# Last pair's small copies moved from GpSimd to VectorE and ScalarE, its transposes put ahead of its products, and more projections held back

## The chip, the cores and the metric

The kernel runs on one core of a Trainium2 chip. The metric is the device time of one execution in microseconds (us): the median of three runs, beside one further execution that was profiled. A profiled execution gives, for each instruction of each engine, its start and its length; all places below are us from the start of that span.

## The reference, cut to what matters

A sequence of 512 positions with 1024 channels goes through two blocks of two layers each, in float32. Only the first block is touched.

```python
h = rms_norm(x, norm_g) * (1 + scale) + shift
a_qkv, a_z, m_cq, m_ckv, m_kr, m_z, merge = split(h @ w_in)
y_a = dilated_mixer(a_qkv, rel_bias) * silu(a_z)      # 3 groups x 8 heads
y_m = mla_mixer(m_cq, m_ckv, m_kr, ...) * silu(m_z)   # 16 heads, causal
g_a, g_m = split(sigmoid(merge))
merged = g_a * (y_a @ w_out_a) + g_m * (y_m @ w_out_b)
x = x + gate * (merged @ w_o)
```

In `dilated_mixer` each of 8 heads has three attentions (window and stride 128/1, 512/4, 2048/16) whose results are mixed by a softmax over their three log-sums. So the weight of each probability needs a small exchange between the three groups, whose queries lie in different orders.

## The kernel before, in words

Every product with a weight matrix is made in three float32r passes (high x high, high x low, low x high: lines 259 to 261), and so one projection of 128 columns over 1024 channels is 24 MATMULs of 128x512, "24 products" below. Weights come as a stream of chunks of up to 1024 columns (512 KB) by DMAs that SyncE issues (line 1642) into four raw buffers. ScalarE casts a chunk to its high part (line 1658) and VectorE makes the low part (line 1659), three chunks ahead of their use. The load of chunk n+4 waits until both have read chunk n. Some chunks (`w_ada`, 32 of them in the first layer's attention) are no weights for TensorE: VectorE reduces each by itself (line 642, 1024 columns).

The order of the program is fixed when it is built. `Order.weave` merges three streams of items: `sc` (scores, softmax, and the small exchange), `tm` (scaling, transposes, products with the values) and `fill` (projections that TensorE can do meanwhile). An item may say that it comes at least so much planned time behind another (`after`); among those that are ready the stream that is furthest behind its share goes first. `hold` counts for `fill` as work already done, so a larger `hold` leaves more projections for the end. Each engine runs its own instructions strictly in that order.

The first weave of a layer is the dilated attention: four pairs of heads (`hp` 0 to 3). For each pair:

- four `scores` items (matmuls in line 795, VectorE's bias and maximum in line 801, ScalarE's exponentials in line 807);
- `combine`: `gather` (18 small copies between partitions, lines 819 and 822, GpSimd), `weigh` and `share` (lines 829 to 843, small VectorE work and one exponential), and 17 small copies back (lines 844 and 847, GpSimd);
- `scale` (line 861, VectorE, multiplies the probabilities by the copied factors), `turn` (transposes, line 870, copied out in line 872 by VectorE or ScalarE) and `mix` (products with the values, line 890).

The fill of this weave holds the next pair's projections, the first heads of the second attention (`heads(0)` and `heads(1)`, with four GpSimd additions in line 1004 that need VectorE's line 571, and copies in lines 1001 and 1008) and five gate projections. In the first layer, `bias_rows2` follows the weave: one DMA of 4088 KB between two DRAM tables, issued by GpSimd (line 605, `rows<-dt`).

The second weave is the second attention (MLA), eight pairs `j` of heads: scores (line 1036), `scale` (1053), `turn` (1061, copied out in 1063), `mix` (1074), the last step of a pair in line 1078. Behind it come the splits of the eight results (`split_ym`, lines 239 and 240), and then for each of 8 blocks a gate projection and the product with `w_out_b`.

Of the kernel before, what the change touches and what calls it, by code (L numbers as in the profile page):

```python
# [17 lines left out]
P = 128  # L18
S = 512
D = 1024  # L20
KD = D // P
DEPTH = 2
NEG = -1e30
HOLD = 20000
NG = 5
DC = 1500
DF = 6000
DT = 5000
# [31 lines left out]
O_MG = O_MZ + 1024  # L60
# [129 lines left out]
class Kernel:  # L190
# [479 lines left out]
    def first_layer(self, l):  # L670
        nc = self.nc
        st = self.st
        get = lambda name: (lambda inputs: inputs[name][l])
        w_in = get("w_in")
# [133 lines left out]
            return Item(1300, fn)  # L808


        def combine(hp):
            v5 = lambda x: x.rearrange("p (v g h b) -> p v g h b", v=2, g=3, h=2)
            v4 = lambda x: x.rearrange("p (g h b) -> p g h b", g=3, h=2)

            def gather(_):
                u = st["u", hp] = self.small(48)
                uv, ml = v5(u), v5(st["ml", hp])
                for v in range(2):
                    nc.gpsimd.tensor_copy(uv[:, v, 0], ml[:, v, 0])
                for b in range(4):  # L820
                    for p in range(4):
                        nc.gpsimd.tensor_copy(uv[32 * p:32 * p + 32, :, 1:3, :, b], ml[32 * b:32 * b + 32, :, 1:3, :, p])

            def weigh(_):
                uv = v5(st["u", hp])
# [8 lines left out]
            def share(_):  # L834
                uv, e = v5(st.pop(("u", hp))), st.pop(("e", hp))
                le, s = self.small(24), self.small(8)
                nc.vector.tensor_tensor(v4(le), uv[:, 1], v4(e), ALU.mult)
                nc.vector.tensor_tensor(s, le[:, 0:8], le[:, 8:16], ALU.add)
                nc.vector.tensor_tensor(s, s, le[:, 16:24], ALU.add)
                nc.vector.reciprocal(s, s)  # L840
                cf = st["cf", hp] = self.small(24)
                cv, ev = v4(cf), v4(e)
                nc.vector.tensor_tensor(ev, ev, s.rearrange("p (h b) -> p h b", h=2).unsqueeze(1).to_broadcast([P, 3, 2, 4]), ALU.mult)
                nc.gpsimd.tensor_copy(cv[:, 0], ev[:, 0])
                for b in range(4):
                    for p in range(4):
                        nc.gpsimd.tensor_copy(cv[32 * b:32 * b + 32, 1:3, :, p], ev[32 * p:32 * p + 32, 1:3, :, b])
            out = [Item(0, gather)]
            out.append(Item(0, weigh, after=[(out[0], 4000)]))
            out.append(Item(0, share, after=[(out[1], 1500)]))  # L850
            return out

# [74 lines left out]
        for hp in range(4):  # L927
# [8 lines left out]
            c[0].after.append((s[3], DC))  # L936
            t = {(h2, b): turn(hp, h2, b) for b in range(4) for h2 in range(2)}
            f = [scale(hp, b) for b in range(4)]
            f[0].after.append((c[-1], DF))
            for b in range(4):  # L940
                t[0, b].after.append((f[b], DT))
            m = [mix(hp, b) for b in range(4)]
# [27 lines left out]
    def first_rest(self, l, sc, tm, fill):  # L970
# [12 lines left out]
        def oa_evac(ps, f):  # L983
            y = self.t()
            self.gated(y, st.pop("sg"), ps)
            st["A", f] = y
            if f == 7:
                for i in range(4):
                    st.pop(("ya", i))
        out_a = []  # L990
        for f in range(8):
            out_a.append(self.proj(w_in, rng(O_MG + f * P, P), D, H, ga_evac) + self.proj(get("w_out_a"), rng(f * P, P), 512, lambda: [st["ya", i] for i in range(4)], lambda ps, f=f: oa_evac(ps, f)))
# [104 lines left out]
        for j in range(8):  # L1097
# [24 lines left out]
            m[3].after.append((gate[-1], MG))  # L1122
            tail[j] = m[3]
            sc += spaced(s, MS) + f
            tm += t[0]
            for k in range(4):
                tm += (t[k + 1] if k < 3 else []) + [m[k]]

        for j in range(6):
            first = next(i for i in fill if i is done[j + 2])  # L1130
# [2 lines left out]
        out = []  # L1133
# [4 lines left out]

        def ob_evac(ps, f):
            y = self.t()  # L1140
            self.gated(y, st.pop("sg"), ps)
            nc.vector.tensor_tensor(y, y, st.pop(("A", f)), ALU.add)
            st["mg"].append(self.split(y))
            if f == 7:
                st.pop("yms")
                st.pop("h")
# [3 lines left out]
            st["mg"] = []  # L1150
        out += [Item(0, split_ym), Item(0, begin)]
        for f in range(8):
            out += self.proj(w_in, rng(O_MG + D + f * P, P), D, H, ga_evac)
            out += self.proj(get("w_out_b"), rng(f * P, P), D, lambda: st["yms"], lambda ps, f=f: ob_evac(ps, f))

        def x_load(_):
# [585 lines left out]
```

## Time and profile before

| | |
|---|---|
| median of three runs | 3296.12 us (3291.93 to 3296.24) |
| profiled execution, its own time | 3293.89 us |
| its span | 3292.0 us |
| TensorE (PE) busy | 3222.0 us, 98% of the span |
| VectorE (DVE) busy | 1793.2 us, 54% |
| ScalarE (ACT) busy | 1272.4 us, 39% |
| GpSimd (POOL) busy | 394.0 us, 12% |
| mean DMA rate | 103 GB/s |

A row of the timeline reads: start in us, length in us, engine, line, operation, output<-input, shape, how many were merged into the row; in brackets the time that the engine stood idle before it and who ended that wait. A row of the waits names who waited for whom: us in total, times, longest. "PEclk" is the clock granted to TensorE, 1.00 for its full 2.4 GHz and 0.50 for 1.2 GHz.

### The profile page before, as it was taken

Reading aid. Unit: us, or ns where it says so; the run is one execution under the profiler, and the core shown is the slowest. Engines: PE = TensorE matmul, PEld = TensorE weight load, DVE = VectorE, ACT = ScalarE, POOL = GpSimd, SP = SyncE. Lnnn points to the kernel's source line nnn. Section 1 sums busy time; section 2 is a strip of 40 time slices with the busy share of each in tenths; the row PEclk is TensorE's granted clock in tenths of the full one; section 3 lists DMA queues with packets and bytes.
Section 4 is the critical chain, followed back from the end, with each engine's and each line's share of the span. In section 5 each row is a group of like instructions: output and inputs, shape, how many; then the busy total and the mean of one; then the engine's idle time right before and its main releaser. Section 6 shows DMA issues by size and latency. Waiting matters only on the chain.

```text
span 3292.0 us, 40715 instructions
## 1 busy us (share of the span) xinstructions
PE 3222.0 (98%) x15488; PEld 2596.7 (79%) x15488; DVE 1793.2 (54%) x3660; ACT 1272.4 (39%) x2433; POOL 394.0 (12%) x651
## 2 busy tenths in 40 slices
PE   7989989999999999999999999999999999999998
PEld 5868767799887677877788878888877788888886
DVE  7556766565456765576634555333666535463333
ACT  3344444344444443454433333223454423242222
POOL 3033301020122010200005110000000024000000
PEclk8999999999999999999999999999999999999999
DMA  6464632264321122332222332332322223322322
GB/s 221 134 170 152 130 80 73 82 197 144 96 72 58 55 69 82 120 124 86 74 91 82 109 115 97 93 102 83 131 92 85 77 83 104 125 92 89 110 84 70
DMA packets 105123, 340.20 MB, mean 103 GB/s; under 512 B 14132, under 2 KB 17380, under 8 KB 104928
## 3 DMA queue, kind: packets, MB, share of 16 engines
q1 hardware_dynamic: 94464, 309.90, 28.9%
q0 software_dynamic: 10464, 27.72, 3.5%
q8 instruction: 121, 1.98, 0.3%
q14 instruction: 74, 0.61, 0.1%
HBM read 329.04 MB, written 16.35 MB: 105 GB/s over the span
## 4 chain that ended last, share of the span: by engine, by line
PE 84%; DVE 6%; issue 3%; ACT 3%; DMA 2%; POOL 1%; SPq 0%; DVEq 0%; ACTq 0%; POOLq 0%
PE ps L259 24%; PE ps L260 24%; PE ps L261 24%; PE ps L1036 2%; DVE lo L1659 1%; PE ps L1074 1%; PE ps L1368 1%; PE ps L1353 1%; PE ps L1061 1%; DMA rows<-dt 1%; PE ps L302 1%; ACT hi L1658 1%; PE ps L303 1%; PE ps L304 1%; PE ps L890 1%
## 5 line engine op out<-in xcount | busy, mean ns | idle before, releaser
L259 PE MATMUL ps<-t,hi 128*128 128x512 f32 (+1 forms) x3904 | 1537.1, 394 | 18.3 <-DVE sm L801 6.7
L260 PE MATMUL ps<-t,hi 128*128 128x512 f32 (+1 forms) x3904 | 1503.1, 385 | 0.7 <-DVE t L240 0.7
L261 PE MATMUL ps<-t,lo 128*128 128x512 f32 (+1 forms) x3904 | 1502.9, 385 | 0.0
L1659 DVE TENSOR_TENSOR lo<-raw,hi 128x1024 fp32r<-128x1024 f32 (+3 forms) x563 | 666.5, 1186 | 723.7 <-ACT hi L1658 723.4
L259 PEld LDWEIGHTS ps<-t,hi 128*128 128x128 f32 x3904 | 735.1, 188 | 178.3 <-issue 11.5
L261 PEld LDWEIGHTS ps<-t,lo 128*128 128x128 f32 x3904 | 734.7, 188 | 148.3
L260 PEld LDWEIGHTS ps<-t,hi 128*128 128x128 f32 x3904 | 735.5, 188 | 145.8 <-issue 6.7
L1658 ACT CAST hi<-raw 128x1024 fp32r<-128x1024 f32 (+5 forms) x567 | 551.7, 975 | 238.0 <-PE ps L260 156.2
L239 ACT CAST t<-t 128x512 fp32r<-128x512 f32 x154 | 91.1, 620 | 382.3 <-DVE t L1560 174.6
L240 DVE TENSOR_TENSOR t<-t,t 128x512 fp32r<-128x512 f32 x154 | 105.7, 710 | 104.9 <-ACT t L239 104.9
L1042 ACT ACTIVATE p<-p,sm 128x128 f32<-128x128 f32 (+3 forms) x128 | 71.9, 562 | 156.5 <-DVE sm L1041 155.4
L1330 ACT ACTIVATE p<-p,sm 128x256 f32<-128x256 f32 (+1 forms) x128 | 72.0, 562 | 144.9 <-DVE sm L1329 143.7
L807 ACT ACTIVATE p<-p,sm 128x128 f32<-128x128 f32 (+1 forms) x192 | 79.7, 417 | 103.6 <-DVE sm L804 103.5
L302 PE MATMUL ps<-hi,t 128*128 128x512 f32 (+1 forms) x272 | 104.3, 383 | 11.8 <-ACT t L242 11.5
L303 PE MATMUL ps<-hi,t 128*128 128x512 f32 (+1 forms) x272 | 102.0, 375 | 1.1 <-DVE t L243 1.1
L304 PE MATMUL ps<-lo,t 128*128 128x512 f32 (+1 forms) x272 | 100.9, 371 | 0.0
L1436 ACT ACTIVATE t<-ps 128x512 f32<-128x512 f32 x48 | 28.7, 598 | 171.3 <-PE ps L261 171.0
L1463 POOL TENSOR_TENSOR c<-c 128x527 f32<-128x527 f32 (+3 forms) x40 | 51.8, 1295 | 336.0 <-ACT c L1459 334.0
L1036 PE MATMUL ps<-c,t 128*128 128x128 f32 (+3 forms) x256 | 90.0, 441 | 0.4 <-DVE t L1001 0.4
L1004 POOL TENSOR_TENSOR t<-t,t 64x512 f32<-64x512 f32 x32 | 42.5, 1342 | 357.0 <-DVE t L571 249.5
L302 PEld LDWEIGHTS ps<-hi,t 128*128 128x128 f32 x272 | 67.4, 248 | 19.3 <-ACT t L242 14.8
L1560 DVE TENSOR_TENSOR t<-ps,t 128x512 f32<-128x512 f32 x38 | 26.3, 692 | 101.4 <-PE ps L261 101.4
(227 smaller groups left out, 2767.4 us busy)
## 6 DMA issues: line engine op xcount, KB each, us to landing
raw<-in_w_dram SPq DMA_DIRECT2D x511, 512.0 KB, 3.3
raw<-in_w_dram SPq DMA_DIRECT2D x33, 384.0 KB, 3.0
raw<-in_w_dram SPq DMA_DIRECT2D x32, 320.0 KB, 2.9
xd<-t SPq DMA_DIRECT2D x24, 256.0 KB, 4.7
t<-xd POOLq DMA_DIRECT2D x24, 256.0 KB, 5.2
bias<-rows POOLq DMA_DIRECT2D x32, 192.0 KB, 2.7
rows<-dt POOLq DMA_DIRECT2D x1, 4088.0 KB, 43.9
raw<-in_w_dram SPq DMA_DIRECT2D x10, 256.0 KB, 2.7
```

What stands on the lines that cost most here:

```text
L239: nc.scalar.copy(hi, y)
L240: nc.vector.tensor_tensor(lo, y, hi.bitcast(F32), ALU.subtract)
L259: mm(out, lhsT=w[0], rhs=x[0], start=start, stop=False)
L260: mm(out, lhsT=w[0], rhs=x[1], start=False, stop=False)
L261: mm(out, lhsT=w[1], rhs=x[0], start=False, stop=stop)
L302: mm(ps, lhsT=xh, rhs=hi[:, s], start=k == 0, stop=False)
L303: mm(ps, lhsT=xl, rhs=hi[:, s], start=False, stop=False)
L304: mm(ps, lhsT=xh, rhs=lo[:, s], start=False, stop=k == kt - 1)
L807: nc.scalar.activation(pr[:, s], pr[:, s], AF.Exp, bias=nm[:, g, h2, b:b + 1], accum_out=ml[:, 1, g, h2, b:b + 1])
L1036: nc.tensor.matmul(ps[:, :n], lhsT=st["q", h][:, b * P:(b + 1) * P], rhs=self.kh[h % 4][:, :n], start=True, stop=True)
L1658: nc.scalar.copy(hi[:, :n], src[:, :n])
L1659: (nc.gpsimd if chunks[c][1][0].aside else nc.vector).tensor_tensor(lo[:, :n], src[:, :n], hi[:, :n].bitcast(F32), ALU.subtract)
```

## The change

In the last pair of the dilated attention (`hp` 3, in both layers) the 35 small copies of `combine` alternate between VectorE and ScalarE, and three planned distances of that pair become shorter: 4000 to 2000 from `gather` to `weigh`, 6000 to 2500 from `share` to `scale`, the rest stays. `HOLD`, the hold of the first weave, goes from 20000 to 30000. In the MLA weave the gate projections of the first two output blocks (`NB` = 2) are appended to the fill, their results kept until they are used, and in the last pair (`j` 7) all transposes come ahead of all products with the values.

```diff
-HOLD = 20000
+HOLD = 30000
+NB = 2
...
+        def copiers(hp):
+            while True:
+                yield from [nc.gpsimd.tensor_copy] if hp < 3 else [nc.vector.tensor_copy, nc.scalar.copy]
...
+                copies = copiers(hp)
                 for v in range(2):
-                    nc.gpsimd.tensor_copy(uv[:, v, 0], ml[:, v, 0])
+                    next(copies)(uv[:, v, 0], ml[:, v, 0])
                 for b in range(4):
                     for p in range(4):
-                        nc.gpsimd.tensor_copy(uv[32 * p:32 * p + 32, :, 1:3, :, b], ml[32 * b:32 * b + 32, :, 1:3, :, p])
+                        next(copies)(uv[32 * p:32 * p + 32, :, 1:3, :, b], ml[32 * b:32 * b + 32, :, 1:3, :, p])
...
-                nc.gpsimd.tensor_copy(cv[:, 0], ev[:, 0])
+                copies = copiers(hp)
+                next(copies)(cv[:, 0], ev[:, 0])
...
-            out.append(Item(0, weigh, after=[(out[0], 4000)]))
+            out.append(Item(0, weigh, after=[(out[0], 4000 if hp < 3 else 2000)]))
...
-            f[0].after.append((c[-1], DF))
+            f[0].after.append((c[-1], DF if hp < 3 else DF - 3500))
...
+        def gb_evac(ps, f):
+            st["gb", f] = self.sigmoid2(ps)
+
+        gates_b = [self.proj(w_in, rng(O_MG + D + f * P, P), D, H, lambda ps, f=f: gb_evac(ps, f)) for f in range(8)]
...
-            tm += t[0]
-            for k in range(4):
-                tm += (t[k + 1] if k < 3 else []) + [m[k]]
+            if j < 7:
+                tm += t[0]
+                for k in range(4):
+                    tm += (t[k + 1] if k < 3 else []) + [m[k]]
+            else:
+
+                tm += sum(t, []) + m
+        fill += sum(gates_b[:NB], [])
...
-            out += self.proj(w_in, rng(O_MG + D + f * P, P), D, H, ga_evac)
+            out += gates_b[f] if f >= NB else []
```

What this does to the order of the program is shown at three places of the first layer, all in the last pair of the dilated attention. In the changed kernel the line numbers are higher: 870, 880 and 890 become 878, 888 and 898; 1004 becomes 1016, 605 becomes 606, 1659 becomes 1676, 642 becomes 643, 861 becomes 869, 259 to 261 become 260 to 262.

TensorE where the first transposes of the pair (`ps<-c,p`) begin, before:

```order
L260 MATMUL ps_3301<-t_554,hi_3114 128x512
L261 MATMUL ps_3301<-t_553,lo_3115 128x512
L870 MATMUL ps_3330<-c_110,p_2814 128x128 x3
L870 MATMUL ps_3336<-c_110,p_2814 128x128 x3
L870 MATMUL ps_3348<-c_110,p_2885 128x128 x4
L870 MATMUL ps_3355<-c_110,p_2885 128x128 x4
L880 LDWEIGHTS c_108
L880 MATMUL ps_3362<-c_108 128x512
L890 MATMUL ps_3362<-t_3334,t_859 64x128
```

and the same place with the change:

```order
L878 MATMUL ps_3234<-c_110,p_2837 128x128 x3
L878 MATMUL ps_3240<-c_110,p_2837 128x128 x3
L878 MATMUL ps_3252<-c_110,p_2901 128x128 x4
L878 MATMUL ps_3259<-c_110,p_2901 128x128 x4
L260 MATMUL ps_3227<-t_366,hi_3069 128x512
L261 MATMUL ps_3227<-t_367,hi_3069 128x512
L262 MATMUL ps_3227<-t_366,lo_3070 128x512
```

From the last scores of the pair to these transposes TensorE had 114 products (rows 1408 to 1521 of its order) and has 72 (rows 1384 to 1455); 66 products now stand between the transposes and the products with the values (24, 18 and 24), where there were none. The pair's last scores themselves come 24 products earlier. In pairs 0 to 2 the 114 become 102. The second layer has the same pattern.

GpSimd around the large DMA (`rows<-dt`), before: the pair's copies (`sm<-sm`), then the DMA.

```order
L819 COPY sm_3125<-sm_2804 128x8 x2
L822 COPY sm_3125<-sm_2804 32x2x4 x16
L844 COPY sm_3215<-sm_3192 128x8
L847 COPY sm_3215<-sm_3192 32x4 x16
L605 DMA rows_3434<-dt_840 2048x1x511
```

with the change: the four additions of the second attention's first heads, then the DMA.

```order
L1016 TENSOR_TENSOR t_3036<-t_2986,t_2987 64x512
L1016 TENSOR_TENSOR t_3039<-t_2986,t_2987 64x512
L1016 TENSOR_TENSOR t_3080<-t_2986,t_2987 64x512
L1016 TENSOR_TENSOR t_3083<-t_2986,t_2987 64x512
L606 DMA rows_3434<-dt_840 2048x1x511
```

The additions stood ahead of the pair's bias loads before. So the DMA is no longer held by the pair's copies.

VectorE between the exchange and the first scaling of the pair (`p<-p,sm`), before:

```order
L843 TENSOR_TENSOR sm_3192<-sm_3192,sm_3210 128x24
L505 SCALAR_TENSOR_TENSOR t_3240<-t_3241,ps_3184 128x512
L642 ISA t_3246,c_84<-raw_3170,held_85 128x1024
L642 ISA c_84 128x1
L1659 TENSOR_TENSOR lo_3251<-raw_3174,hi_3250 128x128
L505 SCALAR_TENSOR_TENSOR t_3279<-t_3280,ps_3254 128x512
L861 TENSOR_SCALAR p_2814<-p_2814,sm_3215 128x128 x6
```

with the change:

```order
L852 COPY sm_3133<-sm_3110 128x8
L855 COPY sm_3133<-sm_3110 32x4 x8
L506 SCALAR_TENSOR_TENSOR t_3158<-t_3159,ps_3102 128x512
L643 ISA t_3164,c_84<-raw_3067,held_85 128x1024
L643 ISA c_84 128x1
L643 ISA t_3168,c_84<-raw_3092,held_85 128x1024
L643 ISA c_84 128x1
L1676 TENSOR_TENSOR lo_3173<-raw_3096,hi_3172 128x1024
L869 TENSOR_SCALAR p_2837<-p_2837,sm_3133 128x128 x6
```

Half of the copies now stand in VectorE's queue, and three chunks of 1024 columns (two for line 643, one for line 1676) come right ahead of the first scaling, where there were one of 1024 and one of 128. Between the pair's last scores (line 801, now 802) and `weigh`, VectorE's queue has in this order: two copies for `heads(0)` (lines 1013 and 1020), its 9 copies of `gather`, a split of 1024, two copies for `heads(1)`, one line 643, a split of 1024. Before, these four copies, one more of line 642 and one more split stood ahead of the last scores, and behind them came two evacuations of products (line 505), two splits and three of line 642.

## Rows read from the trace of the kernel before

**Rows 1.** The page: busy time of each engine, share and instructions.

```profile
PE 3222.0 (98%) x15488; PEld 2596.7 (79%) x15488; DVE 1793.2 (54%) x3660; ACT 1272.4 (39%) x2433; POOL 394.0 (12%) x651
```

**Rows 2.** Waits of TensorE over the whole span.

```profile
PE ps L1061 <- DVE sm L1038: 8.5, 2, 7.5
...
PE ps L259 <- DVE t L571: 4.3, 3, 1.7
```

**Rows 3.** Timeline of TensorE, first layer: pairs 0 and 3, second weave's start.

```profile
225.80 2.42 PE L870 MATMUL ps<-c,p 128*128 128x128 f32 x13 [1.07 <-DVE p L861]
...
354.06 1.15 PE L795 MATMUL ps<-t,t 64*128 64x256 f32 x12
...
381.27 0.30 PE L870 MATMUL ps<-c,p 128*128 128x128 f32 x1
383.00 1.10 PE L870 MATMUL ps<-c,p 128*128 128x128 f32 x5 [1.43 <-DVE p L861]
...
395.12 0.49 PE L1036 MATMUL ps<-c,t 128*128 128x128 f32 x2
...
425.64 2.39 PE L1061 MATMUL ps<-c,p 128*128 128x128 f32 x10 [7.47 <-DVE sm L1038]
```

**Rows 4.** Windows: us, busy us by engine, PEclk, DMA share, GB/s.

```profile
380.00:400.00 20.00, 17.27 (x120) 13.55 (x119) 14.68 (x42) 5.95 (x12) 3.78 (x16) 0.83 0.91 123
```

**Rows 5.** Timeline of layer 1's last pair on TensorE, VectorE and GpSimd.

```profile
1025.55 1.15 PE L795 MATMUL ps<-t,t 64*128 64x256 f32 x12
...
1052.60 1.69 PE L870 MATMUL ps<-c,p 128*128 128x128 f32 x14
...
1060.50 0.49 PE L1036 MATMUL ps<-c,t 128*128 128x128 f32 x2
...
1034.80 0.17 DVE L804 TENSOR_SCALAR sm<-sm 128x3 f32<-128x3 f32 x1
...
1048.60 2.57 DVE L861 TENSOR_SCALAR p<-p,sm 128x128 f32<-128x128 f32 x12
```

**Rows 6.** Timeline of GpSimd, first layer, last pair.

```profile
347.89 3.86 POOL L1004 TENSOR_TENSOR t<-t,t 64x512 f32<-64x512 f32 x3 [26.02 <-DVE t L571]
...
367.45 7.59 POOL L822 COPY sm<-sm 32x8 f32<-32x8 f32 x16
...
378.87 4.56 POOL L847 COPY sm<-sm 32x4 f32<-32x4 f32 x15
383.37 1.04 POOL L605 DMA_DIRECT2D rows<-dt  x1
```

**Rows 7.** Timeline of VectorE, first layer, last pair.

```profile
366.16 0.17 DVE L804 TENSOR_SCALAR sm<-sm 128x3 f32<-128x3 f32 x1
...
371.23 1.22 DVE L642 CUSTOM_DVE_ANT_0 t<-raw,held 128x1024 bf16<-128x1024 f32 x1
...
376.40 0.16 DVE L829 TENSOR_TENSOR sm<-sm 128x8 f32<-128x8 f32 x1
...
382.65 2.89 DVE L861 TENSOR_SCALAR p<-p,sm 128x128 f32<-128x128 f32 x11 [1.53 <-POOL sm L847]
```

**Rows 8.** DMA issues, windows 156:176 and then 383:430: KB each, median us to landing.

```profile
raw<-in_w_dram SPq DMA_DIRECT2D x5, 512.0 KB, 14.0
...
rows<-dt POOLq DMA_DIRECT2D x1, 4088.0 KB, 43.9
raw<-in_w_dram SPq DMA_DIRECT2D x3, 512.0 KB, 26.6
```

**Rows 9.** Groups by line, shapes apart: count, busy us, mean ns.

```profile
L1659 DVE TENSOR_TENSOR lo<-raw,hi 128x1024 fp32r<-128x1024 f32 x459 | 579.0, 1264 | 588.0 <-ACT hi L1658 587.7
...
L1001 DVE COPY t<-ps 64x512 f32<-64x512 f32 x16 | 11.1, 693 | 7.0 <-ACT t L1001 6.7
```

**Rows 10.** Timeline of the first layer's MLA end, TensorE and VectorE.

```profile
585.81 3.37 PE L1061 MATMUL ps<-c,p 128*128 128x128 f32 x14
...
593.78 4.89 DVE L240 TENSOR_TENSOR t<-t,t 128x512 fp32r<-128x512 f32 x8
```

More of the change, by code (lines that the diff above doesn't have):

```diff
@@ L843, in share @@
                 nc.vector.tensor_tensor(ev, ev, s.rearrange("p (h b) -> p h b", h=2).unsqueeze(1).to_broadcast([P, 3, 2, 4]), ALU.mult)
-                nc.gpsimd.tensor_copy(cv[:, 0], ev[:, 0])
+                copies = copiers(hp)
+                next(copies)(cv[:, 0], ev[:, 0])
                 for b in range(4):
                     for p in range(4):
-                        nc.gpsimd.tensor_copy(cv[32 * b:32 * b + 32, 1:3, :, p], ev[32 * p:32 * p + 32, 1:3, :, b])
+                        next(copies)(cv[32 * b:32 * b + 32, 1:3, :, p], ev[32 * p:32 * p + 32, 1:3, :, b])
             out = [Item(0, gather)]
-            out.append(Item(0, weigh, after=[(out[0], 4000)]))
+            out.append(Item(0, weigh, after=[(out[0], 4000 if hp < 3 else 2000)]))
             out.append(Item(0, share, after=[(out[1], 1500)]))
@@ L1140, in ob_evac @@
             y = self.t()
-            self.gated(y, st.pop("sg"), ps)
+            self.gated(y, st.pop(("gb", f)), ps)
             nc.vector.tensor_tensor(y, y, st.pop(("A", f)), ALU.add)
```

## Prediction

> **What bounds the kernel now.** I read the page first: TensorE is busy for 3222.0 of 3292.0 us, 98% [rows 1]. The change leaves out no matmul, so it can only win back time in which TensorE stands idle or runs at its lower clock, about 70 us in all, and can only lose by adding some. The second view is the list of TensorE's waits, which I located in the timeline. Two that lie inside the changed stretches are large: 7.5 us for a scale of the second attention (line 1061 for VectorE's line 1038), and 1.7 us in each layer for line 571 [rows 2]. The third view is the timeline of the first layer. The last pair's transposes begin at 381.27 and stall for 1.43 us until VectorE has scaled, and the 7.47 us stall comes at 425.64, after the weave [rows 3]. Between 380 and 400 the granted clock is 0.83 on average [rows 4], so a third of that stretch was at 1.2 GHz: some 3.4 us of work lost. The fourth view is the same place in the second layer, the clean case. TensorE ends the last scores at 1026.70 (1025.55 + 1.15), runs its 114 products until 1052.60, and the whole end of the pair takes 7.9 us, to 1060.50, without a wait [rows 5]. So a product costs 25.9 / 114 = 0.227 us, and in this layer the end of the dilated attention has nothing to win but the 1.7 us at line 571.
>
> **The cover that goes.** From the last scores to the first transposes TensorE has 72 products in place of 114: 16.3 us in place of 25.9. In pairs 0 to 2 it has 102, so 2.7 us less. There, only pair 0 of the first layer already stalls, 1.07 us [rows 3], while its copies stay on GpSimd, so I add 2.7 us; the others begin to scale well ahead of their transposes, as pair 3 of the second layer does, by 4 us [rows 5].
>
> **What the copies give.** In the second layer the first scaling came 1048.60 - 1026.70 = 21.9 us after the scores, with 0.4 us for the two operations that the first transpose needs: 22.3 us of need against 25.9 of cover [rows 5]. In the first layer it was 383.0 - 355.2 = 27.8 us against 25.9 [rows 3]. GpSimd's copies take 7.6 and 4.6 us [rows 6]. On VectorE a small operation takes 0.16 us [rows 7]; I take the same for ScalarE, which the rows don't show for this shape. 9 copies on each in parallel come to 1.5 us a time. If all of the difference were on the path, need would fall by about 9 us, to 19 in the first layer and (fewer products behind it) about 16 in the second. That is the lower bound of the stall: 3 us and 0.
>
> The other bound follows VectorE's queue, as the order shows it. In the first layer VectorE ended the last scores at 366.3, 11 us behind TensorE [rows 3, 7]: it is already behind there. In the second the lag was 1035.0 - 1026.7 = 8.3 us [rows 5]. Between the scores and the first scaling it now has: waiting for the last exponentials and two copies of line 1001's kind (together 1.7), 9 copies (1.5), two more of 0.69 [rows 9] (1.4), splits of 1024 at 1.26 [rows 9] (three: 3.8), `weigh` and `share` (1.9, the eight small operations of 0.16 to 0.2 and one exponential between them), 9 copies (1.5), an evacuation (0.7) and two scalings (0.4): 12.9 us, and in the first layer three of line 642 at 1.22 [rows 7] on top: 16.6 us. Need is then 8.3 + 12.9 = 21.2 us in the second layer, a stall of 4.9, and 11 + 16.6 = 27.6 in the first, a stall of 11. The copies buy little, for VectorE's own queue is what is late, and they stand in it. I take this bound, since each item in it is a measured instruction in a fixed order. A stall of this length brings a stretch at the lower clock, as in rows 4; I charge 1 us for it in the second layer.
>
> **The large DMA moves.** This is the largest term. `rows<-dt` was held back to 383.37 by the pair's copies on GpSimd [rows 6], at the moment when TensorE began its end of the pair, which needs no weights. It took 43.9 us, and weight loads issued while it ran took 26.6 us to land [rows 8]. That is also what made the 7.47 us stall: the split of a late chunk stood ahead of a scaling in VectorE's queue. Now the DMA stands behind the four additions of line 1004, which follow line 571 ahead of the last scores. Their time in the changed kernel: VectorE ended the scores at 366.3; four copies (2.8), a split (1.3) and one of line 642 (1.2) move behind them, so they end near 361.1, and line 571 near 359.1. Four additions at 3.86 / 3 = 1.29 us [rows 6] end at 364.3, and the DMA starts then, 19 us earlier.
>
> Now which loads fall under it? Ahead of the first scaling VectorE has to pass six chunks after the scores. A load is issued when the chunk four before it has been read. The last two, needed by a line 642 and by the split right ahead of the scaling, are issued when the first two have been read: 361.1 + 1.7 + 1.5 + 1.3 = 365.6, and 1.4 + 1.2 later, 368.2. Both come just after the DMA's start. At 26.6 us they land at 392.2 and 394.8; with a split and two scalings the transposes can begin at 396.5. TensorE is there at 355.2 - 24 x 0.227 + 16.3 = 366.1. So it stands idle for some 30 us.
>
> After that it has the 66 products (15.0) and the end's own 7.9 us [rows 5], and 1.7 us for half a stretch like that of rows 4: 421.1 in place of 395.12 [rows 3], **+26.0 us**. Later in the tail further chunks come under the DMA, but 24 products lie ahead of them and it ends near 408; I charge nothing, at most 8 us.
>
> What comes back: the second attention now starts with the DMA gone, so the 7.47 us stall and about 1.5 us of low clock behind it disappear, **-9.0**. The loads of the second weave's start were otherwise on time.
>
> **The end of MLA.** Before, 14 transposes took 3.37 us with VectorE's scaling between them [rows 10], where 14 took 1.69 elsewhere [rows 5]. With projections to fill, 1.7 us per layer come back. But the first gate used to cover the splits of `split_ym`: these take 4.89 us for 8 [rows 10]. Now the product with `w_out_b` begins at once and waits for the step of line 1078 and the first split, about 1.3 us; then splits (0.61 each) keep ahead of three products (0.68). For both layers together I take **-1.0**, between 0 and -3.4.
>
> **The sum**, in us: +26.0 - 9.0 (first layer, pair 3 and after), +2.7 (pair 0), -1.7 (the wait for line 571, which I kept in the 366.1, if fewer projections in flight free the buffers), and in the second layer +4.9 + 1.0 - 1.7 = +4.2, and -1.0: +21.2. The profiled execution took 3293.89, so **3315**. The median of the runs is 3296.12, 0.07% above the profiled one; I stay with the sum.
>
> **Rivals.** (a) *The queues share.* Loads under the earlier, smaller DMAs of 1020 KB landed in 14.0 us [rows 8], not 26.6. Then they land by 382.2, scaling begins at 383.9, the tail ends at 408.5, 12.6 us less than above: 3302.5. For it: two other cases in the same trace. Against: the very same DMA gave 26.6. The Trainium skill (DMA: Bandwidth & Descriptors, section Queues, rings and completion order) speaks for it: each DMA engine takes turns between its queues, a packet from each, so a load should not wait behind a long transfer. By it this rival's 3302.5 would be the outcome at most; the 26.6 us speaks against it, the 14.0 for it.
>
> (b) *The loads are in time, VectorE's queue alone decides.* If the additions are later or VectorE faster by some 4 us, both loads are issued ahead of the DMA. The stall is 11 us, the tail ends at 366.1 + 11 + 24.6 = 401.7, 19.4 us below the sum: 3296.
>
> (c) *Faster.* The copies were the path, and the moved DMA harms nothing. The tail ends at 355.2 - 5.4 + 19.2 + 22.9 = 391.9, -3.2 against before; then -9.0, +2.7, -1.7, -1.7 and -1.0: -13.9, so 3280. It decides at one point: whether VectorE can begin to scale within 16 to 19 us of TensorE's last scores. VectorE's lag of 8 to 11 us speaks against it; for it speaks that VectorE did wait for GpSimd's copies in the first layer, 1.53 us [rows 7].
>
> (d) *Worse.* Loads land one after another under the DMA, and the chunks behind the scaling stall the tail again, up to 8 us: 3323.
>
> **Chances.** Sum 0.56 (3305 to 3322); (a) 0.18 (3298 to 3305); (b) 0.09 (3291 to 3300); (c) 0.12 (3272 to 3289); (d) 0.05 (to 3332). A change of 0.2%, 6.6 us, is about what a measurement of this kernel can tell from none: faster below 3289.5, slower above 3302.7. Slower: 0.56 + 0.05 + half of (a), 0.70. Same: the other half of (a) and most of (b), 0.17. Faster: (c) and a rest of (b), 0.13. The range leaves out (c) and the upper end of (d): 3289 to 3326.
>
> **What would show it.** In the first layer: the DMA's issue near 364 in place of 383, an idle TensorE of about 30 us before line 878 around 366 to 396, released by the scaling, with ScalarE's cast and line 643 waiting for `raw` there, and no 7 us stall at line 1073 afterwards. In the second layer a stall of 2 to 8 us at the same place, without a DMA in it. Pair 0 of the first layer: a stall near 3.8 us. At the ends of MLA no stall among the transposes and one of about 1 us at the first product with `w_out_b`. The forecast is wrong if the DMA is issued later than about 370, if loads under it land in a few us, or if VectorE's last scores in the changed kernel come much earlier than 361, which would mean that it is not its queue that is late.

## The result and the profile after

The changed kernel takes 3330.92 us, the median of four runs (3328.92 to 3333.0), against 3294.95 us for the kernel before (four runs, 3291.93 to 3296.24): a ratio of 1.011, 95% interval 1.0094 to 1.0126. It is slower by 36 us, where I had forecast 21. The profiled execution has a span of 3327.1 us, 35.1 more than before.

TensorE is busy about as long as before (3222.0 us there [rows 1]), so what was lost is waiting:

```profile
PE 3219.7 (97%) x15488; PEld 2598.2 (78%) x15488; DVE 1793.5 (54%) x3696; ACT 1280.1 (38%) x2467; POOL 380.4 (11%) x581
```

The timeline of TensorE of the changed kernel, at the places that answer to [rows 3] and [rows 5]: pair 0, the last pair's transposes, the former 7.47 us stall, two places in the weave of MLA, its end, and the last pair of the second layer.

```profile
222.48 0.33 PE L878 MATMUL ps<-c,p 128*128 128x128 f32 x1 [1.72 <-DVE p L869]
...
403.94 3.27 PE L878 MATMUL ps<-c,p 128*128 128x128 f32 x14 [35.16 <-DVE p L869]
...
452.77 1.47 PE L1073 MATMUL ps<-c,p 128*128 128x128 f32 x10 [1.07 <-DVE sm L1050]
...
484.03 0.50 PE L260 MATMUL ps<-t,hi 128*128 128x512 f32 x1 [1.05 <-DVE t L973]
...
529.71 0.70 PE L1048 MATMUL ps<-c,t 128*128 128x256 f32 x2 [0.97 <-DVE sm L1050]
...
631.46 0.50 PE L261 MATMUL ps<-t,hi 128*128 128x512 f32 x1 [0.99 <-DVE t L241]
...
1070.59 3.20 PE L878 MATMUL ps<-c,p 128*128 128x128 f32 x14 [7.76 <-DVE p L869]
```

One stall of 35.16 us is as long as the whole difference; the other gains and losses nearly cancel, and a table further down adds them up. TensorE came to it at 403.94 - 35.16 = 368.8. What ended it is read on VectorE, GpSimd and the DMA queues. First VectorE's timeline of the same kernel:

```profile
375.93 1.22 DVE L643 CUSTOM_DVE_ANT_0 t<-raw,held 128x1024 bf16<-128x1024 f32 x1
...
394.39 1.23 DVE L643 CUSTOM_DVE_ANT_0 t<-raw,held 128x1024 bf16<-128x1024 f32 x1 [17.24 <-DMA raw<-in_w_dram]
...
402.47 1.22 DVE L1676 TENSOR_TENSOR lo<-raw,hi 128x1024 fp32r<-128x1024 f32 x1 [6.84 <-ACT hi L1675]
403.61 2.57 DVE L869 TENSOR_SCALAR p<-p,sm 128x128 f32<-128x128 f32 x12
```

Then GpSimd's timeline, its issue of the large transfer, which stood at 383.37 [rows 6]:

```profile
362.19 1.05 POOL L606 DMA_DIRECT2D rows<-dt  x1
```

And the line of the weight loads (1659) for those issued between 366.9 and 371.5, with the least, median and longest time from issue to landing:

```profile
L1659 SPq DMA_DIRECT2D raw<-in_w_dram x3: 328/328/328, 367.6 to 371.0; - x3
...
DMA to landing us min/median/max: 26.8/31.5/35.5
```

The reader is to see a chain. The load issued at 367.6 lands 26.8 us later, at 394.4, and starts line 643. The next one lands 31.5 us after its issue; ScalarE's cast of it releases line 1676 at 402.47. Only behind that does VectorE reach the scaling, 403.61, that TensorE waits for.

Why the loads land so late is seen in the packets of the two queues, q0 the transfer's and q1 the loads' (packets, MB, share of the 16 DMA engines). From 368 to 382 us, with three loads issued by 371 and a fourth at 377, only the transfer's queue moves packets:

```profile
q0 software_dynamic: 165, 1.01, 100.2%
```

From 384 to 402 both move, packet for packet:

```profile
q0 software_dynamic: 353, 2.16, 64.1%
q1 hardware_dynamic: 353, 1.31, 37.0%
```

What stops the loads' queue in the first stretch is not shown. While TensorE stands there its clock falls (window of the stall: length, busy us by engine, granted clock, DMA share, GB/s):

```profile
366.00:404.00 38.00, 1.99 (x7) 1.03 (x7) 12.13 (x31) 6.11 (x16) 0.00 (x0) 0.56 1.03 137
```

### The profile page after: what moved, and what is told of

It reads as the page before. It is cut to its first block, busy times and chain, and to the rows that moved or that the text cites. A ratio compares the mean times of both kernels' runs of the same rounds, so it can differ in the third digit from the quotient of the medians.

```text
span 3327.1 us, 40721 instructions
## 1 busy us (share of the span) xinstructions
PE 3219.7 (97%) x15488; PEld 2598.2 (78%) x15488; DVE 1793.5 (54%) x3696; ACT 1280.1 (38%) x2467; POOL 380.4 (11%) x581
## 4 chain that ended last, share of the span: by engine, by line
PE 82%; DVE 7%; ACT 4%; issue 4%; DMA 2%; POOL 1%; DVEq 0%; ACTq 0%; POOLq 0%
PE ps L260 24%; PE ps L261 23%; PE ps L262 23%; DVE lo L1676 2%; PE ps L1048 2%; PE ps L1385 1%; PE ps L1086 1%; DMA raw<-in_w_dram 1%; PE ps L1370 1%; ACT hi L1675 1%; DMA rows<-dt 1%; PE ps L1073 1%; PE ps L878 1%; ACT p L808 1%; PE ps L303 1%
## 5 line engine op out<-in xcount | busy, mean ns | idle before, releaser
L260 PE MATMUL ps<-t,hi 128*128 128x512 f32 (+1 forms) x3904 | 1538.5, 394 | 11.3 <-ACT t L240 3.9
L260 PEld LDWEIGHTS ps<-t,hi 128*128 128x128 f32 x3904 | 735.2, 188 | 171.7 <-issue 13.3
L1675 ACT CAST hi<-raw 128x1024 fp32r<-128x1024 f32 (+6 forms) x567 | 551.9, 976 | 258.7 <-PE ps L261 156.3
L506 DVE SCALAR_TENSOR_TENSOR t<-t,ps 128x512 f32<-128x512 f32 x56 | 38.4, 685 | 80.9 <-ACT t L501 44.0
```

The costliest lines, as they stand in the source:

```text
L260: mm(out, lhsT=w[0], rhs=x[0], start=start, stop=False)
L1675: nc.scalar.copy(hi[:, :n], src[:, :n])
```

## The experiments

The kernel before is itself uneven: in single runs beside the first eight experiments it took 3283.28 and 3283.19 us, in 21 runs beside the last ones 3288.61 to 3298.08. So I compare the experiments at one place of their traces: where the first product of line 302 (303 in kernels with the changed numbering) of the second block starts, behind all that the edits touch. In the kernel before that is 1405.7 us, in the changed kernel 1441.4, so the whole loss, 35.7 us, lies ahead of it. The first scores of the block, near its start, begin between 190.2 and 193.6 us in these traces (with HOLD at 20000, where they lie ahead of every edit, between 190.7 and 193.6), so a difference under 3 us of the places says nothing by itself. Counted from those first scores (last column) the two traces of the kernel before agree within 0.4 us, and so do the two of it with the transfer late. The places by run:

| kernel | 4088 KB transfer issued | second block starts | stall, 1st layer | stall, 2nd layer | from the first scores |
|---|---|---|---|---|---|
| before | 383.4 | 1405.7 | 1.43, then 7.47 | none | 1212.5 |
| before, once more | 384.1 | 1405.8 | 1.43, then 6.55 | none | 1212.2 |
| changed | 362.2 | 1441.4 | 35.16 | 7.76 | 1248.9 |
| changed, transfer late | 515.9 | 1419.6 | 10.90 | 7.75 | 1229.4 |
| changed, copies on GpSimd | 379.9 | 1432.6 | 10.75 and 1.50, then 4.89 and 3.83 | 4.96 and 1.95 | 1240.8 |
| changed, transfer late, HOLD 20000 | 510.5 | 1407.3 | 7.23 | 1.46 | 1216.1 |
| changed, transfer late, old lags | 514.5 | 1411.6 | 8.51 | 4.61 | 1221.0 |
| before, copies as changed | 357.7 | 1421.9 | 27.27 | none | 1230.8 |
| before, copies as changed, transfer late | 499.5 | 1400.0 | 3.37 | none | 1207.2 |
| before, transfer early | 357.2 | 1422.9 | 26.78 | none | 1232.2 |
| before, transfer late (two kernels) | 493.5, 494.9 | 1393.9, 1395.3 | 1.43 | none | 1203.2, 1203.1 |
| before, MLA end as changed | 383.3 | 1410.6 | 1.57, then 2.90 and 6.11 | none | 1217.7 |
| before, MLA end as changed, transfer late | 505.7 | 1406.1 | 1.57, later 3.19 | none | 1213.2 |

"Late" means one edit:

```diff
-        if l == 0:
-            add([Item(0, self.bias_rows2)])
...
+            if l == 0 and j == 3:
+                fill.append(Item(0, self.bias_rows2))
```

**The changed kernel, transfer late.** Theory 1 is that of the prediction's largest term, loads that land late under the transfer; theory 2 its rival, VectorE's own queue.

> The changed kernel with only the large DMA (rows<-dt) moved: it is issued in the middle of the second attention of the first layer (pair 3 of 8) instead of ahead of it. Theory 1 (the stall is the loads that land late under this DMA): the 35 us stall at the first transposes of the last pair shrinks to the time that VectorE's own queue needs, about 10 us, and the whole takes about 24 us less, near 3306. Theory 2 (VectorE's queue, with the copies in it, is what is late, and the loads only wait in its shadow): the stall stays above 25 us and the time near 3330.

3300.86 us. TensorE's timeline, and the load line between 360 and 375:

```profile
377.68 2.63 PE L878 MATMUL ps<-c,p 128*128 128x128 f32 x11 [10.90 <-DVE p L869]
...
1045.83 3.27 PE L878 MATMUL ps<-c,p 128*128 128x128 f32 x14 [7.75 <-DVE p L869]
```

```profile
DMA to landing us min/median/max: 3.1/3.3/4.6
```

The same loads land in 3.3 us, and the stall is 10.90 in place of 35.16. The transfer's place is worth 1441.4 - 1419.6 = 21.8 us here, 19.5 counted from the first scores. The profiled executions differ by more, 28 us: some 5 us went behind all that the edits touch (see the experiment with the transfer early). The 10.90 us is what theory 2 has right, and the second layer's stall is the same without any transfer.

**The kernel before with the copies alone.** The copies as changed; HOLD, lags and the MLA end as before. Against the changed kernel:

```diff
-HOLD = 30000
+HOLD = 20000
...
-            out.append(Item(0, weigh, after=[(out[0], 4000 if hp < 3 else 2000)]))
+            out.append(Item(0, weigh, after=[(out[0], 4000)]))
...
-            f[0].after.append((c[-1], DF if hp < 3 else DF - 3500))
+            f[0].after.append((c[-1], DF))
...
-NB = 2
+NB = 0
...
-            if j < 7:
+            if True:
```

> The kernel before with only the engine of the last pair's 35 small copies changed to VectorE and ScalarE; hold, distances, transposes and gates as before. Theory 1: without the copies on GpSimd the large DMA is issued near 360 instead of 383, the chunks ahead of the scaling come under it, TensorE stalls some 24 us at 381, and with the 7.5 us stall afterwards gone the whole is 8 to 14 us slower than before, near 3306; the second layer has no stall. Theory 2: with 114 products of cover VectorE is in time, the copies save a little, and the time is 3290 to 3295.

3309.21 us. GpSimd, rid of the copies, issues the transfer at 357.72. VectorE's and TensorE's timelines:

```profile
385.70 1.23 DVE L643 CUSTOM_DVE_ANT_0 t<-raw,held 128x1024 bf16<-128x1024 f32 x1 [13.48 <-DMA raw<-in_w_dram]
...
393.28 1.23 DVE L643 CUSTOM_DVE_ANT_0 t<-raw,held 128x1024 bf16<-128x1024 f32 x1 [6.35 <-DMA raw<-in_w_dram]
```

```profile
406.77 3.22 PE L878 MATMUL ps<-c,p 128*128 128x128 f32 x14 [27.27 <-DVE p L869]
```

Theory 1's stall, 27.27 us where I had said some 24, though the cover is the old one, and none in the second layer.

**The changed kernel with its 35 copies back on GpSimd.**

```diff
-                yield from [nc.gpsimd.tensor_copy] if hp < 3 else [nc.vector.tensor_copy, nc.scalar.copy]
+                yield from [nc.gpsimd.tensor_copy]
```

> The changed kernel with only the 35 copies put back on GpSimd; hold, shorter distances, transposes and gates as changed. Theory 1: the DMA is held by the copies again and issued when the scaling can begin, so the stall at the first transposes is what the chain over GpSimd leaves over the 72 products, 10 to 13 us in the first layer and 6 to 8 in the second; the 66 products behind it now meet late loads, up to 10 us more; 3310 to 3320. Theory 2: GpSimd's copies are slower, so both stalls are longer than with the copies on VectorE and ScalarE, over 35 and over 8 us, and the time is above 3331.

3321.06 us, a little over theory 1's range, with the two late stalls it had named (line 1048's wait is behind a cast):

```profile
377.57 0.48 PE L878 MATMUL ps<-c,p 128*128 128x128 f32 x1 [10.75 <-DVE p L869]
...
413.54 0.79 PE L260 MATMUL ps<-t,hi 128*128 128x512 f32 x1 [4.89 <-DVE t L506]
423.14 6.61 PE L1048 MATMUL ps<-c,t 128*128 128x256 f32 x10 [3.83 <-ACT t L973]
...
1057.85 0.47 PE L878 MATMUL ps<-c,p 128*128 128x128 f32 x1 [4.96 <-DVE p L869]
```

It also prices the copies where no transfer runs. In its second layer TensorE ended the last scores at 1036.34 and could begin to transpose at 1057.85: a need of 21.5 us. With the copies on VectorE and ScalarE (the changed kernel with the transfer late) it was 1045.83 - 1021.51 = 24.3. But with GpSimd only the first of the 14 transposes comes that early; the others wait for its second round of copies (TensorE, then VectorE):

```profile
1060.28 3.08 PE L878 MATMUL ps<-c,p 128*128 128x128 f32 x13 [1.95 <-DVE p L869]
```

```profile
1059.93 2.38 DVE L869 TENSOR_SCALAR p<-p,sm 128x128 f32<-128x128 f32 x11 [2.13 <-POOL sm L855]
```

The two stalls make 6.91 us against one of 7.75, so in this layer the engine of the copies changes less than 1 us.

**The kernel before, its copies untouched, with the transfer ahead of them.**

```diff
             def gather(_):
+                if l == 0 and hp == 3:
+                    self.bias_rows2(None)
```

> The kernel before, its copies still on GpSimd, with one edit: the 4088 KB transfer is issued ahead of the last pair's copies, near 360 us in place of 383 us. Theory 1 (loads that land late under the transfer make the stall; the copies themselves cost nothing): a stall of 20 to 30 us before the first layer's last products, the later one of 7.47 us gone, and a time 16 to 26 us over the kernel before. Theory 2 (the copies in VectorE's queue make it): the stall stays near 1.4 us, and the time within 4 us of the kernel before.

3304.26 us. GpSimd's and TensorE's timelines:

```profile
357.16 1.06 POOL L605 DMA_DIRECT2D rows<-dt  x1
```

```profile
405.70 0.45 PE L872 MATMUL ps<-c,p 128*128 128x128 f32 x1 [26.78 <-DVE p L863]
...
443.28 1.47 PE L1063 MATMUL ps<-c,p 128*128 128x128 f32 x10 [1.07 <-DVE sm L1040]
```

No copy was moved, no lag, no HOLD: one DMA issued 26 us earlier makes the 26.78 us stall, and the later one is gone. This is theory 1 by itself. From 1422.9 on this kernel and the first experiment needed about 5 us less than the others up to their last product of line 302 (953.5 us against 958.6 in the kernel before, profiled once more). No edit lies there. In the other twelve traces one split of VectorE, beside eight additions of GpSimd, takes 9.3 us, where splits of its size take 1.26 [rows 9]; TensorE then stalls for 2.9 us and has a stretch at half the clock. In the kernel before:

```profile
1916.44 9.34 DVE L1659 TENSOR_TENSOR lo<-raw,hi 128x1024 fp32r<-128x1024 f32 x1 [2.78 <-ACT hi L1658]
```

In these two kernels the same split takes 1.9 us, and TensorE does not stall. Why it meets the additions otherwise there is not shown.

**The kernel before with the copies, transfer late.** The diff of "copies alone" and that of "late" together.

> The kernel before with the copies of the last pair on VectorE and ScalarE alone, and the 4088 KB transfer issued in the middle of the MLA stage. Theory 1 (weight loads that land late under the large transfer make the first layer's stall): with the transfer gone from there no stall over 3 us at the products of the first layer's last pair, and a time within 4 us of the kernel before of the same chip or up to 10 us under it. Theory 2 (VectorE's queue, made longer by the copies): the stall stays over 20 us, and the time lies 20 to 26 us over the kernel before.

3287.39 us. The stall:

```profile
384.62 3.22 PE L878 MATMUL ps<-c,p 128*128 128x128 f32 x14 [3.37 <-DVE p L869]
```

Theory 1, nearly: 3.37 us where I had said under 3, and 4.2 us over the kernel before of the same round (3283.19) where I had said 4. The four kernels of copies and transfer make a square. Counted from the first scores, the copies cost 1207.2 - 1203.2 = 4.0 us with the transfer late and 1230.8 - 1232.2 = -1.4 with it early; the transfer costs 29.0 us early against late without the copies and 23.6 with them. So the copies' own price is small, some 4 us, and it vanishes where the loads decide.

**HOLD and the lags, one at a time, transfer late.** What is left of the changed kernel's stalls then comes from VectorE's need and TensorE's cover. The first kernel has, of the diff of "copies alone", the hunk of HOLD, the other the two of the lags (these two are all the planned distances that the change shortens, not three), each on top of "late":

> The changed kernel with the 4088 KB transfer in the middle of the MLA stage and HOLD back at 20000; lags and order as changed. With HOLD at 30000 the stalls that were left were 10.90 us (first layer) and 7.75 us (second). Theory A (HOLD took the cover: the projections that stood between the scores and the products of the last pair): both fall under 3 us, and the time lies about 20 us under that run, within 3 us of the kernel before or under it. Theory B (the shorter lags put the products too early): both stay over 6 us, and the time stays 14 to 18 us over the kernel before.

> The changed kernel with the 4088 KB transfer in the middle of the MLA stage and the two lags of the last pair back at 4000 and 6000; HOLD stays at 30000. Theory A (HOLD took the cover): the stalls of 10.90 and 7.75 us stay over 6 us each, and the time 14 to 18 us over the kernel before. Theory B (the shorter lags put the products too early): both fall under 3 us, and the time lies within 3 us of the kernel before or under it.

3294.50 and 3298.67 us. TensorE's timeline of the first, then of the second:

```profile
379.77 3.22 PE L878 MATMUL ps<-c,p 128*128 128x128 f32 x14 [7.23 <-DVE p L869]
...
1045.60 2.52 PE L878 MATMUL ps<-c,p 128*128 128x128 f32 x14 [1.46 <-DVE p L869]
```

```profile
381.71 3.22 PE L878 MATMUL ps<-c,p 128*128 128x128 f32 x14 [8.51 <-DVE p L869]
...
1046.57 3.17 PE L878 MATMUL ps<-c,p 128*128 128x128 f32 x14 [4.61 <-DVE p L869]
```

Neither theory holds alone, in the stalls or in time (11.3 and 15.5 us over the kernel before of the same round). Counted from the end of the last scores to TensorE's arrival at 0.227 us a product [rows 5], the second layer's cover is 73 products with both changed, 85 with HOLD back, 97 with the lags back, 114 with both back. Both take cover away, and either alone leaves a stall. But the need moves too: from the last scores to the first transpose it is 24.3 us with both changed, 20.7 with HOLD back and 26.6 with the lags back. So HOLD takes 2.7 us of cover and adds 3.6 us of need; the lags take 5.4 us of cover and save 2.3 us of need. Where HOLD adds need is VectorE's queue: with HOLD at 30000 four of line 572 (571 before) stand right ahead of the pair's last scores, as in the changed kernel's second layer; with HOLD at 20000 they stand ahead of the scores before those.

```profile
1050.67 2.80 DVE L572 TENSOR_TENSOR t<-ps,held 32x512 f32<-32x512 f32 x4
```

Counted from the first scores HOLD is worth 13.3 us (1229.4 - 1216.1) and the lags 8.4 (1229.4 - 1221.0).

**The kernel before, profiled once more.**

> The kernel before, unchanged, profiled once more, because it took 3283.3 and 3283.2 us beside the experiments and 3292 to 3296 us earlier. If the spread is the time at which the large transfer meets the weight loads: a shorter later stall than 7.47 us, or none, and about 9 us less between 381 and 460 us. If it is a general difference of the chips: the same stalls, and 10 us less spread over the span or ahead of 200 us.

3293.14 us, the same stalls, the later one 6.55 us. So this execution doesn't explain the two runs at 3283; that stays open.

**The kernel before with only the transfer late**, first in one run and then in five:

> The kernel before with only the large DMA moved to the middle of the second attention of the first layer. Theory 1: the 7.5 us stall after the dilated attention and the low clock behind it go, 8 to 10 us, near 3286, if four raw buffers are enough there for loads that take some 27 us; if they are not, the stall only moves and the time is 3292 to 3297. Theory 2 says nothing else here.

> The kernel before with the 4088 KB transfer in the middle of the MLA stage alone. Theory 1 (weight loads late under that transfer cost the kernel before its later stall and two stretches at half the clock): 2 to 10 us under the kernel before in every round, and no stall over 2 us after the first layer's last pair. If the transfer costs nothing where it was: within 2 us of the kernel before.

3281.46 us in the one run, 1.8 under a single run of the kernel before; in five runs 3283.67 (3282.89 to 3284.68) against 3294.99, a ratio of 0.9966, interval 0.9954 to 0.9979. This beats both kernels, by 11.3 and 47 us; why the single pair differs by so much less is the open question of the two runs at 3283. TensorE's timeline, and the window from 380 to 430 of the kernel before profiled once more and of this one:

```profile
415.72 1.47 PE L1061 MATMUL ps<-c,p 128*128 128x128 f32 x10 [1.07 <-DVE sm L1038]
```

```profile
380.00:430.00 50.00, 39.20 (x204) 29.30 (x203) 35.84 (x104) 18.53 (x44) 7.03 (x18) 0.86 0.92 157
```

```profile
380.00:430.00 50.00, 45.04 (x248) 31.66 (x247) 40.70 (x120) 21.09 (x52) 5.78 (x14) 0.97 0.25 80
```

Where the time comes from: 6.55 - 1.07 = 5.5 us of stall, and up to (0.97 - 0.86) x 50 = 5.5 us of clock (an estimate from above, since part of the low clock falls into the stall); counted from the first scores the whole is some 9 us. The transfer is not cheap at its new place either. Its DMA issues, 495 to 540, and then those of 355 to 400, with the number of loads, KB each and the median us to landing:

```profile
rows<-dt POOLq DMA_DIRECT2D x1, 4088.0 KB, 44.4
raw<-in_w_dram SPq DMA_DIRECT2D x5, 512.0 KB, 22.9
raw<-in_w_dram SPq DMA_DIRECT2D x1, 192.0 KB, 22.0
```

```profile
raw<-in_w_dram SPq DMA_DIRECT2D x10, 512.0 KB, 4.2
raw<-in_w_dram SPq DMA_DIRECT2D x2, 256.0 KB, 4.0
raw<-in_w_dram SPq DMA_DIRECT2D x1, 448.0 KB, 3.3
```

Under the transfer six loads are issued in 45 us, one in 7.5 us; four buffers are then a lead of some 30 us, more than the 22.9 that a load takes. Between 355 and 400, where the changed kernel has its transfer (362 to 407), it is 14 in 45 us, counting one of 64 KB that isn't shown: one in 3.2, a lead of 13 us. That the lead decides is worked out, not tried by itself. The moment counts too. In the three kernels with the transfer late and the old MLA end, a load is issued 0.9 us behind the transfer, moves its first packets 2.7 or 2.8 us after that, and TensorE has no stall over 0.3 us under it. In the eleven other traces the first load comes 3.3 to 5.4 us behind the transfer and moves nothing for 13.3 to 15.6 us.

**The MLA end alone**, at the old place of the transfer and with it late. Of the change, these hunks:

```diff
+NB = 2
...
-                tm += (t[k + 1] if k < 3 else []) + [m[k]]
+            if j < 7:
...
+                tm += sum(t, []) + m
+        fill += sum(gates_b[:NB], [])
...
+            out += gates_b[f] if f >= NB else []
```

> The kernel before with the MLA end alone as changed: two gate projections held for the end, the last pair of heads' transposes ahead of its products. Forecast: 1 us under the kernel before over both layers. Rival (the new short stalls of 0.74, 1.05, 0.97 and 0.99 us in each layer cost as much as they give, or more): 0 to 4 us over it.

> The kernel before with the 4088 KB transfer in the middle of the MLA stage and the MLA end as changed; copies on GpSimd, old lags, HOLD 20000. If both edits add up: 3 to 11 us under the kernel before. If the MLA end costs as much as it gives or more: the time of the transfer's move alone, or up to 4 us over that.

3297.52 us in 11 runs, ratio 1.0006 (0.9997 to 1.0015): no difference that can be told, between 1.0 us less and 4.9 more. With the transfer late 3294.68, ratio 0.9999 (0.999 to 1.0008): the 11 us that the transfer's move gives are gone, which none of my two cases had. TensorE's timeline of the second:

```profile
446.68 0.33 PE L1073 MATMUL ps<-c,p 128*128 128x128 f32 x1 [0.74 <-ACT t L973]
448.06 0.50 PE L260 MATMUL ps<-t,hi 128*128 128x512 f32 x1 [1.05 <-DVE t L973]
493.73 0.70 PE L1048 MATMUL ps<-c,t 128*128 128x256 f32 x2 [0.97 <-DVE sm L1050]
...
552.72 1.98 PE L1086 MATMUL ps<-t,t 128*64 128x512 f32 x4 [3.19 <-DVE t L1075]
602.05 0.50 PE L261 MATMUL ps<-t,hi 128*128 128x512 f32 x1 [0.99 <-DVE t L241]
```

Four short stalls, 3.75 us in each layer, are in both kernels with this end; the 3.19 us stall is only in that with the late transfer. The whole is 1406.1 - 1395.3 = 10.8 us, 10.1 counted from the first scores. From the first product of the first layer's MLA stage (line 302 or 303) to that of the next layer it takes 332.0 us in place of 324.7, so 7.3 us lie there: the first load comes 4.1 us behind the late transfer (0.9 in the kernel without this end), and of the stalls 4.5 us (0.83, 0.49 and 3.19) come between 546 and 553, as the transfer ends. The second layer's MLA stage, where no transfer runs, takes 347.4 in place of 345.0, and the same 347.4 against 345.0 in the two kernels with the transfer at its old place. So 2.4 us is what this end costs in a layer, short stalls and a 3.4 us stretch at half the clock (from 1112 here), less what the transposes give back.

## Why the prediction was wrong

The direction, the place and the mechanism were right, the size was not: +36.0 us against +21.2, outside the range (to 3326). The step that failed is the time to landing: I gave two loads the same median. The traces, cut at the first product of line 302 (303) of each stage, show where the other 14.5 us lie:

| stretch | forecast | measured |
|---|---|---|
| start to the first layer's MLA stage | 26.0 + 2.7 - 1.7 = +27.0 | 429.29 - 395.36 = +33.93 |
| first layer's MLA stage, to the next layer | -9.0 - 0.5 = -9.5 | 325.69 - 332.24 = -6.55 |
| from there to the second layer's MLA stage | +4.2 | 340.47 - 333.14 = +7.33 |
| second layer's MLA stage | -0.5 | 345.94 - 344.93 = +1.01 |
| sum | +21.2 | +35.72 |

- *The large DMA moves.* Right: issued at 362.2 where I had 364, one idle stretch of TensorE from 368.8 (forecast 366.1), released by the scaling behind line 643 and a cast that wait for `raw`, and no 7 us stall afterwards. That one moved DMA makes it is shown by the kernel with that edit alone.
- *The term that failed most: the landing of the two loads.* I gave both the 26.6 us of [rows 8]. The first took 26.8, the second, issued right behind it, 31.5, a third 35.5. Issues 2 us later, a second load 5 us longer and ScalarE's cast of it (1.0 us, from 401.39), which I had left out, put the first transpose at 403.94 in place of 396.5, and the tail's end at 429.05 in place of 421.1: **7 to 8 us**. This is the first half of rival (d), loads one after another, to which I gave 0.05; its second half, new stalls behind the scaling, did not come. The 26.6 was a median of three loads; the row of each was to be had. It was right for the first load behind the transfer, as in six more traces with a transfer in the first layer's attention or at its end (24.3 to 27.2 us); loads issued 1.1 to 2.3 us behind such a load took 30.7 to 32.8.
- *VectorE's queue in the second layer.* Right that the copies give little, since they stand in VectorE's own queue: their two rounds took 1.5 and 1.6 us there, as forecast. I had a need of 21.2 us; it was 24.3, and the stall 7.76 in place of 4.9: **2.9 us**, and a stretch of 6.8 us at half the clock, where I had charged 1 us. What was longer is the rest of the queue. VectorE ended the last scores 9.9 us behind TensorE, where I kept the 8.3 of the kernel before, and line 569 and four of line 572 (3.5 us together) now stand right ahead of them. From there to the first transpose it took 14.4 us in place of 12.9: some 3 us more of waiting for ScalarE, and one split less than I had counted. With HOLD back at 20000 the lag is 8.2 us and the need 20.7, so this comes with HOLD, which I had charged only with cover.
- *The end of MLA.* Forecast -1.0 for both layers. The wait at the first product with `w_out_b` came as forecast (0.99 us, I had 1.3), but the held-back gates brought three more short stalls inside the weave, 2.76 us a layer, that I had not looked for. In the changed kernel the second layer's MLA stage took 1.0 us more, and the first layer's 1.0 us more than in the kernels whose 7 us stall is gone (325.7 against 324.7): +2.0 in place of -1.0, **3 us**. The end alone, where a stretch at half the clock follows, puts the second block's start 4.8 us later (1410.6 - 1405.8), though its runs can't tell it from none.
- *What comes back.* The 7.47 us stall went, as forecast. The tail's end comes 33.9 us later than before, and the weight split that starts at 734.02 in the kernel before, behind MLA's end, 27.4 us later: 6.5 us were given back by then, in place of 9.5. With the old MLA end and the transfer at another place (five kernels) the first layer's MLA stage takes 324.6 to 324.7 us, against 332.2 and 331.5 in the two traces of the kernel before. So the stall and the low clock behind it were worth about 7 us and not 9.0; the rest of the difference is the end of MLA.
- *Pair 0.* Forecast +2.7 for the first layer; the two waits there are 1.72 and 0.98 in place of 1.07 [rows 3], so +1.6. The waits for line 571 (1.7 us in each layer) went, as forecast.

Rival (a), by which loads under the transfer land in 14.0 us, is refuted: they took 26.8 to 35.5, and 3.3 with the transfer gone. The Trainium skill (DMA: Bandwidth & Descriptors, section Queues, rings and completion order) says that an engine takes turns between its queues, a packet from each. The trace agrees from 384 to 402 us, 353 packets from each queue; before that, from 368 to 382, it does not (165 packets and none), and this is what (a) missed. Rival (b) is close to what the changed kernel does with the transfer late (stall 10.90, I had 11). Rival (c) needed VectorE to scale within 16 to 19 us of the last scores; the least of any kernel with the changed copies was 1045.17 - 1024.88 = 20.3 us, with HOLD at 20000 in the second layer.

## What to carry to other kernels

An engine's queue also sets when the DMAs behind its work are issued: taking work off GpSimd moved a 4 MB transfer 21 us forward, into a stretch where four buffers lead by some 13 us and a load under it takes 27 or more, and that cost more than the work ever had. So list, for each operation taken off a queue, the transfers queued behind it and the loads that will run under them, and price these one by one, the later ones longer, not by their median. Before tuning around such a transfer, try moving it alone: here that one edit was worth 11 us in five runs (1.8 in a single pair), and everything else together lost time. And a larger hold not only takes cover away, it can also put work ahead of the scores in another engine's queue.

## What had not been expected of the hardware

A load of 512 KB that lands in 3.3 us alone takes 26.8, 31.5 and 35.5 us when three are issued within 3.4 us under one 4088 KB transfer of another queue, and the transfer itself takes 39.5 to 44.8 us in all fourteen traces. One issued at 377.2 took 30.5 us, one at 395.6 still 13.2. The wait has two parts: a first load issued 3.3 to 5.4 us behind the transfer moves no packet for 13.3 to 15.6 us (eleven traces), and then the two queues move as many packets each (353 and 353 from 384 to 402). A load issued 0.9 us behind the transfer moves packets after 2.8 us (three traces), yet lands only after 20.1 to 22.9. A split of VectorE that takes 1.26 us elsewhere took 9.34 beside GpSimd's additions. The clock fell to half in the stall (0.56 from 366 to 404) and, in the second layer, in one of 7.76 us.
